# Hybrid mLSTM and sparse-attention block: another order for the attention step, the compressed branch spread out, 32 small sums moved to GpSimd

## The chip, the core and the metric

The kernel runs on one core of one Trainium2 chip. The metric is device time in microseconds of one execution; less is better. Three runs of the kernel before gave 2147.64, 2150.17 and 2151.10 us, median 2150.17 us. One further execution was recorded by the hardware profiler, and all rows below come from it.

## The reference, cut to what matters

One layer over 256 tokens of width 4096. A wide projection gives the inputs of an mLSTM half and of an attention half; their outputs, gated, go through `w_out`, are added to `x`, and a second gated product is added.

```python
def reference(x, p, norm_w, w_in, ..., w_out, ple_proj, ple_gate):
    h = _rmsnorm(x, norm_w[layer])
    u = h @ w_in[layer]
    ...
    y_ml = hm.reshape(B, S, ML_WIDTH) * jax.nn.sigmoid(ml_o) * jax.nn.silu(ml_z)
    y_ns = _nsa(ns_q, ns_kc, ns_vc, ns_ks, ns_vs, ns_kw, ns_vw, ns_g, ...) * jax.nn.silu(ns_z)
    x = x + jnp.concatenate([y_ml, y_ns], axis=-1) @ w_out[layer]
    x = x + jax.nn.sigmoid(x @ ple_gate[layer]) * (p[layer] @ ple_proj[layer])
```

The attention half (`_nsa`) has 4 groups of 4 heads of width 128. Every query attends three times: to 15 compressed blocks (`sc`, `p_c`, `o_c`), to selected blocks (with 256 tokens all 4 blocks of 64 are selected) and to a window (512, so it too reaches back over all tokens). The three results are added with gates:

```python
    blk = jnp.concatenate([seg[:, :-1], seg[:, 1:]], axis=2) + pe[:, None, :]   # _compress
    ...
    sc = jnp.einsum('bsghd,bcgd->bghsc', qg, kcmp) * scale + bias_c
    p_c = _masked_softmax(sc, dist_c >= 0)
    o_c = jnp.einsum('bghsc,bcgd->bsghd', p_c, vcmp)
    ...
    s = jnp.einsum('bqghd,bgqkd->bghqk', qb, kg) * scale + bias
    pr = _masked_softmax(s, ...)
    ...
    o = gs[..., 0:1] * o_c + gs[..., 1:2] * o_s + gs[..., 2:3] * o_w
```

## The kernel before, in words

The kernel is one long list of units. A unit is one 512 KB weight tile (`raw`, 128x1024 numbers) loaded by SyncE's queue and the matmuls that use it. To keep nearly full precision a tile is split in two: ScalarE writes its high part (`whi`, L1478), VectorE subtracts that from the tile and writes the low part (`wlo`, L1479). A unit of the kind "wide" (L912 to L914) is 12 matmuls of 512 columns: two blocks, two halves of the tokens, three products of high and low parts. Other units ("pair", L1191) use a scheme with fewer products that needs sums of neighbouring weight tiles on VectorE (L1276 to L1280, `raw<-raw`).

The main loop at the end of the program goes through the units in order. In iteration n it first splits unit n+3 (`LOOK` is 3; `whi` and `wlo` have four buffers each), then runs what was put off in `behind`, then issues the matmuls of unit n, then takes one step of each of the queues of generators: `urgent`, `fifo`, and `dry`. All side work (attention, mLSTM, norms, tables) is written as such generators, one step per `yield`. Engines run their instructions in the order of the program, so the place of a step between the units is the place of its instructions on every engine.

The attention of one group is the generator `t_nq`. After the norm it runs 11 steps, one per unit. The eight attention units of the group are the pairs (head h, half t of the queries); t = 0 sees 128 keys, t = 1 sees 256, both for two branches (selected and window) side by side. In step i come, on TensorE, the scores of attention unit i (L582 to L584, into the one PSUM bank `sd0`), the transposes of unit i-2 (L616, into `sd1`), and the products with the values of unit i-3 (L629, into `sd2` for t = 0 and `sd3` for t = 1); on VectorE the bias is added to the scores (L592, it reads `sd0`, so the next scores wait for it), their maximum taken (L594), and the transposed weights of unit i-2 copied (L621); on ScalarE the exponential (L599). `coef` (L604, L605, VectorE) and `scale` (L609, ScalarE) of unit i are put into `behind`: they follow the next iteration's split. Small biased tables `tb` come by DMAs issued on GpSimd's queue (L521).

The compressed branch is a generator inside (`compressed`, L537 to L575): eight small score products into `sd3` (L540), a block-diagonal tile `bd` of the compressed values (cleared by GpSimd, L543, filled by four ScalarE copies, L557), a softmax on VectorE (L548 to L566), two transposes (L571) and at the end one product per half (L632).

Elsewhere `t_xp` (L310) adds the position table `pe` to the transposed inputs of the compression, in 32 VectorE additions of 128x120 numbers, for the 16 units whose matmuls stand in L1004. `t_stat` (L817 and after) turns finished activations into stationary tiles; its `pause` says how many steps pass before the first transposes.

Of the kernel before, what the change touches and what calls it, by code (L numbers as in the profile page):

```python
# [21 lines left out]
NCMP = 15  # L22
# [65 lines left out]
def hymba_block(ctx: ExitStack, tc: tile.TileContext, a, out: bass.AP):  # L88
# [209 lines left out]
    def t_xp():  # L298
        while "ct" not in done:
            yield "wait"  # L300
        for q in range(4):
            if q % 2 == 0:
                both_q = wk.tile([128, 2, 8, 120], F32, tag=f"nat{q // 2}", name="xq")
            xq[q] = both_q[:, q % 2]
            for kv in range(2):
                o = 16 * (q // 2)
                v = held[f"c{kv}"][:, :, o:o + 240].rearrange("p g (b l) -> p g b l", l=16)
                l0 = 8 * (q % 2)
                for g in range(4):
                    nc.vector.tensor_tensor(  # L310
                        xq[q][:, :, kv * 60 + g * 15:kv * 60 + (g + 1) * 15].rearrange("p l b -> p b l"),
                        v[:, g, :, l0:l0 + 8],
                        pe[:, kv, None, 8 * q:8 * q + 8].to_broadcast([128, 15, 8]), op=OP.add)
                if kv:
                    done.add(f"xq{q}")
                yield
# [184 lines left out]
    def t_nq(flag, g):  # L501
# [8 lines left out]
        for t in range(2):  # L510
            r = slice(t * 128, (t + 1) * 128)
            nc.scalar.activation(qh[:, :, r], pp[t], AF.Copy)
            nc.vector.tensor_sub(ql[:, :, r], pp[t], qh[:, :, r])
        units = [(h, t) for t in range(2) for h in range(4)]
        tb = {}

        def load_tb(i):
            h, t = units[i]
            n = 128 * (t + 1)
            tb[i] = wk.tile([128, n], F32, tag="tb", name="tb", bufs=3)  # L520
            nc.gpsimd.dma_start(tb[i], bass.AP(tensor=rext_d.tensor, offset=rext_d.offset + (4 * g + h) * 384 + 1,  # L521
                                               ap=[[1, 128], [1, n]]))

        for i in range(2):
            load_tb(i)
        yield
# [9 lines left out]
        def compressed():  # L536
            pc = side(3, [128, 8, NCMP])  # L537
            for t in range(2):
                for h in range(4):
                    MM(pc[:, 4 * t + h, :], qt[:, h, t * 128:(t + 1) * 128], kct[:, g, :], start=True, stop=True)  # L540
            yield
            bd = cm["bd"] = sqtile([128, 4, 128])
            nc.gpsimd.memset(bd, 0.0)  # L543
            sc = small([128, 8, 32], "sc", 1)
            nc.gpsimd.memset(sc, 0.0)
            scv = sc[:, :, 0:NCMP]
            for t in range(2):
                nc.vector.tensor_tensor(scv[:, 4 * t:4 * t + 4], pc[:, 4 * t:4 * t + 4],  # L548
                                        biasc[:, 8 - 8 * t:23 - 8 * t, 4 * g:4 * g + 4].rearrange("p c h -> p h c"), op=OP.add)
            m8 = small([128, 8], "mx8")  # L550
            nc.vector.tensor_reduce(m8, scv, axis=AX.X, op=OP.max)
            nc.vector.tensor_tensor(scv, scv, m8[:, :, None].to_broadcast([128, 8, NCMP]), op=OP.subtract)
            yield
            nc.scalar.activation(scv, scv, AF.Exp)
            for h in range(4):
                r = slice(32 * h, 32 * h + 32)
                nc.scalar.activation(bd[r, h, :], vcmp[r, g, :], AF.Copy)  # L557
            yield
            sm = small([128, 8], "sm8")
            nc.vector.tensor_reduce(sm, scv, axis=AX.X, op=OP.add)  # L560
            nc.vector.reciprocal(sm, sm)
            nc.vector.tensor_tensor(sm.rearrange("p (t h) -> p t h", t=2), sm.rearrange("p (t h) -> p t h", t=2),
                                    sg4[:, :, 4 * g:4 * g + 4, 0], op=OP.mult)
            nc.vector.tensor_tensor(scv, scv, sm[:, :, None].to_broadcast([128, 8, NCMP]), op=OP.mult)
            for t in range(2):
# [3 lines left out]
            pp = side(3, [128, 2, 128])  # L569
            for t in range(2):  # L570
                nc.tensor.transpose(pp[:, t, :], sc[:, 4 * t:4 * t + 4, :].rearrange("p h c -> p (h c)"), idn)  # L571
            yield
            pct = cm["pct"] = small([128, 2, 128], "pct", 1)
            nc.vector.tensor_copy(pct, pp)
            yield  # L575

        def scores(i):
            h, t = units[i]
            n = 128 * (t + 1)
            psd[i] = side(0, [128, 2, n])  # L580
            r = slice(t * 128, (t + 1) * 128)
            MM(psd[i], qh[:, h, r], kh[:, g, :, 0:n], start=True, stop=False)  # L582
            MM(psd[i], ql[:, h, r], kh[:, g, :, 0:n], start=False, stop=False)
            MM(psd[i], qh[:, h, r], kl[:, g, :, 0:n], start=False, stop=True)  # L584
            if i + 2 < 8:
                load_tb(i + 2)

        def bias_max(i):
            h, t = units[i]
            n = 128 * (t + 1)  # L590
            sb[i] = stile([128, 2, n])
            nc.vector.tensor_tensor(sb[i], psd[i], tb.pop(i)[:, n - 1::-1][:, None, :].to_broadcast([128, 2, n]), op=OP.add)  # L592
            mx[i] = small([128, 2], "mx2", 3)
# [17 lines left out]
        def trans(i):  # L611
            h, t = units[i]
            psd[i] = side(1, [128, 2, t + 1, 128])
            for b in range(2):
                for s in range(t + 1):
                    nc.tensor.transpose(psd[i][:, b, s, :], sb[i][:, b, s * 128:(s + 1) * 128], idn)  # L616

        def copy_pt(i):
            h, t = units[i]
            ptb[i] = pttile([128, 2, t + 1, 128])  # L620
            nc.vector.tensor_copy(ptb[i], psd[i])  # L621

# [20 lines left out]
        for i in range(11):  # L643
# [288 lines left out]
    def add(*gens):  # L932
        fifo.extend(gens)
# [260 lines left out]
    def pair_group(g, w, stat):  # L1194
# [48 lines left out]
        def new_activations(g, chunks, b):  # L1243

            if g < 0:
                add(t_stat([(c, (c * 512 + 2048) % 4096, f"p1_{c}", f"y{c}") for c in chunks], range(16), b, pace=1 + b, pause=1 - b))
            else:
                add(t_stat([(c, c * 512, f"p2_{c}", f"r{c}") for c in chunks], (), b, pace=1 + b, pause=1 - b))
            if b:
# [204 lines left out]

    raws, splits = {}, {}

# [12 lines left out]

    held_raw = [0]  # L1470

# [11 lines left out]
    def split_one(r):  # L1483
# [3 lines left out]
        return hi, lo  # L1487

    def split(n):
        r = raws.pop(n, None)  # L1490
        if n == 0:
# [39 lines left out]
    for n in range(N):  # L1531
        un = units[n]
        late = un.get("late")
# [105 lines left out]
```

## Time and profile before

| | |
|---|---|
| median of three runs | 2150.17 us (2147.64 to 2151.10) |
| the profiled execution's own time | 2147.24 us |
| its span in the profile | 2145.5 us |
| granted TensorE clock, mean | 0.998 of full speed |
| TensorE matmuls busy | 2114.0 us, 99% |
| VectorE busy | 1727.4 us, 81% |
| ScalarE busy | 1218.3 us, 57% |
| GpSimd busy | 42.7 us, 2% |

The time lies 1.74 us above the span. A busy TensorE in this profile has modelled ends: a short matmul's record lasts 0.28 us, while matmuls of 128 columns can pass every 0.11 us, so a record that ends late can hide a piece of a wait. In the rows, `sd<-kh,qh` names the output and inputs of an instruction, "[1.96 <-DVE s L592]" the idle time before it and who ended it.

### The profile page before, as it was taken

The page shows a single profiled execution, that of the slowest core. Times are in us where ns is not written, and L with a number is a line of the kernel's source. Part 1 is how long each engine was busy: PE and PEld are TensorE (multiplying, and loading weights), DVE is VectorE, ACT ScalarE, POOL GpSimd, SP SyncE. Part 2 cuts the span into 40 slices and gives each one's busy share as a digit, 9 for nine tenths or more (in the row PEclk, how much of TensorE's full clock was granted, in tenths as well). Part 3 has the DMA queues.
Part 4 walks back from the last instruction along what each step waited for, and adds up shares of the span by engine and source line. Part 5 has one row for each costly group of instructions (what it writes and reads, how often), then busy time and mean ns, then how long its engine had stood idle before and what let it go on. Part 6 is the DMA issues. An engine that isn't in the chain of part 4 may idle for free.

```text
span 2145.5 us, 27052 instructions
## 1 busy us (share of the span) xinstructions
PE 2114.0 (99%) x9655; PEld 1732.8 (81%) x9655; DVE 1727.4 (81%) x2246; ACT 1218.3 (57%) x1573; POOL 42.7 (2%) x90
## 2 busy tenths in 40 slices
PE   9999999999999999999999999999999999999998
PEld 7877788877777888888888888888888888888887
DVE  7885699566565767869999899888998986988888
ACT  7654455555555555565655556565555555555554
POOL 1000000010000000000000000000000000000000
PEclk9999999999999999999999999999999999999999
DMA  9646756554444455665566566556665665566664
GB/s 370 220 157 233 247 197 208 195 169 145 135 139 147 144 182 177 188 204 177 186 212 223 175 206 220 198 201 241 204 225 179 213 217 167 198 204 221 203 216 145
DMA packets 118759, 423.14 MB, mean 197 GB/s; under 512 B 13906, under 2 KB 14218, under 8 KB 118624
## 3 DMA queue, kind: packets, MB, share of 16 engines
q1 hardware_dynamic: 114272, 409.00, 56.6%
q0 software_dynamic: 4208, 12.40, 2.0%
q8 instruction: 76, 1.25, 0.2%
q14 instruction: 59, 0.48, 0.1%
q10 hardware_dynamic: 144, 0.02, 0.0%
HBM read 417.13 MB, written 4.23 MB: 196 GB/s over the span
## 4 chain that ended last, share of the span: by engine, by line
PE 90%; DVE 6%; ACT 3%; issue 1%; ACTq 0%; DVEq 0%
PE mm L1191 44%; PE sd L1191 28%; PE mm L912 8%; PE mm L914 4%; DVE wlo L1479 3%; ACT whi L1478 1%; ACT s L599 1%; DVE mx L594 1%; PE sd L1004 1%; DVE s L592 1%; PE sd L817 1%; PE sd L629 0%; PE sd L279 0%; PE sd L616 0%; DVE xq L310 0%
## 5 line engine op out<-in xcount | busy, mean ns | idle before, releaser
L1479 DVE TENSOR_TENSOR wlo<-raw,whi 128x1024 fp32r<-128x1024 f32 x848 | 1029.6, 1221 | 353.0 <-ACT whi L1478 338.7
L1478 ACT ACTIVATE whi<-raw 128x1024 fp32r<-128x1024 f32 x848 | 890.2, 1059 | 692.4 <-PE mm L1191 164.9
L1191 PE MATMUL mm<-whi,sh 128*128 128x512 f32 x1221 | 395.2, 393 | 1.4 <-DVE vsw L1092 0.5
L1191 PE MATMUL mm<-wlo,sh 128*128 128x512 f32 x1221 | 390.4, 390 | 1.0 <-DVE wlo L1479 1.0
L1191 PE MATMUL mm<-whi,sl 128*128 128x512 f32 x1221 | 390.4, 390 | 0.0
L1191 PEld LDWEIGHTS mm<-wlo,sh 128*128 128x128 f32 x1221 | 229.3, 188 | 50.2 <-DVE wlo L1479 2.7
L1191 PEld LDWEIGHTS mm<-whi,sh 128*128 128x128 f32 x1221 | 227.5, 188 | 52.3 <-issue 4.1
L1191 PEld LDWEIGHTS mm<-whi,sl 128*128 128x128 f32 x1221 | 229.7, 188 | 48.4
L1191 PE MATMUL sd<-whi,sh 128*128 128x512 f32 x686 | 225.3, 390 | 0.0
L1191 PE MATMUL sd<-whi,sl 128*128 128x512 f32 x686 | 224.9, 389 | 0.0
L1191 PE MATMUL sd<-wlo,sh 128*128 128x512 f32 x686 | 224.9, 389 | 0.0
L912 PE MATMUL mm<-whi,sh 128*128 128x512 f32 x512 | 166.9, 407 | 0.3 <-DVE mv L1092 0.3
L912 PE MATMUL mm<-whi,sl 128*128 128x512 f32 x512 | 158.8, 392 | 0.0
L914 PE MATMUL mm<-wlo,sh 128*128 128x512 f32 x512 | 158.2, 390 | 0.0
L1191 PEld LDWEIGHTS sd<-whi,sl 128*128 128x128 f32 x686 | 128.9, 188 | 27.0
L1191 PEld LDWEIGHTS sd<-wlo,sh 128*128 128x128 f32 x686 | 128.9, 188 | 26.9
L1191 PEld LDWEIGHTS sd<-whi,sh 128*128 128x128 f32 x686 | 128.6, 188 | 26.8
L1191 PE MATMUL sd<-whi,cb 128*128 128x512 f32 x450 | 146.8, 391 | 0.0
L1191 PE MATMUL mm<-whi,cb 128*128 128x512 f32 x390 | 130.7, 391 | 0.0
L914 PEld LDWEIGHTS mm<-wlo,sh 128*128 128x128 f32 x512 | 96.4, 188 | 20.9
L912 PEld LDWEIGHTS mm<-whi,sl 128*128 128x128 f32 x512 | 96.4, 188 | 20.8
L912 PEld LDWEIGHTS mm<-whi,sh 128*128 128x128 f32 x512 | 92.8, 189 | 20.3 <-issue 3.8
(325 smaller groups left out, 1975.7 us busy)
## 6 DMA issues: line engine op xcount, KB each, us to landing
raw<-in_w_gate SPq DMA_DIRECT2D x192, 512.0 KB, 4.2
raw<-in_w_ip SPq DMA_DIRECT2D x159, 512.0 KB, 4.3
raw<-in_w_in SPq DMA_DIRECT2D x128, 512.0 KB, 3.5
raw<-in_w_out SPq DMA_DIRECT2D x128, 512.0 KB, 4.2
raw<-in_ple_gate SPq DMA_DIRECT2D x128, 512.0 KB, 3.5
raw<-in_w SPq DMA_DIRECT2D x16, 512.0 KB, 4.6
u<-in_xt SPq DMA_DIRECT2D x16, 256.0 KB, 7.9
xn<-in_x SPq DMA_DIRECT2D x4, 1024.0 KB, 6.3
```

The costliest lines, as they stand in the source:

```text
L592: nc.vector.tensor_tensor(sb[i], psd[i], tb.pop(i)[:, n - 1::-1][:, None, :].to_broadcast([128, 2, n]), op=OP.add)
L594: nc.vector.tensor_reduce(mx[i], sb[i], axis=AX.X, op=OP.max, negate=True)
L599: nc.scalar.activation(sb[i][:, b], sb[i][:, b], AF.Exp, bias=mx[i][:, b:b + 1], accum_out=sums[i][:, b:b + 1])
L817: nc.tensor.transpose(pp[i // 2][:, i % 2, t * 128:(t + 1) * 128], src[:, t, k:k + 128], idn)
L912: MM(box["ps"][t], s[c][:, k, t * 128:(t + 1) * 128], m[:, j, :], start=st, stop=False)
L914: MM(box["ps"][t], sh[c][:, k, t * 128:(t + 1) * 128], lo[:, j, :], start=False, stop=last)
L1004: MM(o[64 * kv:64 * kv + 60], xq[l // 8][:, l % 8, 60 * kv:60 * kv + 60], raw[:, j, 256 * kv:256 * kv + 256], start=(l == 0), stop=(l == 31))
L1191: MM(acc.t, s, m, start=acc.i == 0, stop=acc.i == acc.n - 1)
L1478: nc.scalar.activation(hi, r, AF.Copy)
L1479: nc.vector.tensor_sub(lo, r, hi)
```

## The change

In `t_nq`:

- The order of attention units is now (h, t) with t fastest, so half 0 and half 1 alternate. The outputs of both halves are complete only at the end: `out_t(0)` moves from step 6 to step 9.
- `tb` is one table of 256 columns per head, used by both halves: four DMAs per group in place of eight.
- In each step a new `split_hi` stands ahead of `bias_max`: ScalarE writes the high part of the unit that the next iteration will split (n+4), ahead of the exponential of the step. `split` finds it done and only subtracts on VectorE, which then comes behind the step's maximum.
- `compressed`: its scores go into the free columns of the score bank of step 0 (`psd[0]`), its transposes into the free columns of step 6's transposes (`psd[4]`); `bd` is filled by four DMAs on GpSimd's queue in place of four ScalarE copies; clearing of `bd` and `sc` and the bias additions move from step 1 to step 0, and the other operations spread over steps 1 to 6.

Elsewhere: the 32 additions of `t_xp` run on GpSimd, and `pause` is 2 in place of 1 for the first two chunks of `t_stat`.

```diff
@@ t_xp
-                    nc.vector.tensor_tensor(
+                    nc.gpsimd.tensor_tensor(
@@ t_nq
-        units = [(h, t) for t in range(2) for h in range(4)]
+        units = [(h, t) for h in range(4) for t in range(2)]
...
+        def load_tb(h):
+            tb[h] = wk.tile([128, 256], F32, tag="tb", name="tb", bufs=3)
...
         def compressed():
-            pc = side(3, [128, 8, NCMP])
+            pc = psd[0][:, 256:256 + 8 * NCMP].rearrange("p (h c) -> p h c", c=NCMP)
...
-            yield
             bd = cm["bd"] = sqtile([128, 4, 128])
             nc.gpsimd.memset(bd, 0.0)
+            for h in range(4):
+                r = slice(32 * h, 32 * h + 32)
+                nc.gpsimd.dma_start(bd[r, h, :], vcmp[r, g, :])
             sc = small([128, 8, 32], "sc", 1)
             nc.gpsimd.memset(sc, 0.0)
...
             nc.scalar.activation(scv, scv, AF.Exp)
-            for h in range(4):
-                r = slice(32 * h, 32 * h + 32)
-                nc.scalar.activation(bd[r, h, :], vcmp[r, g, :], AF.Copy)
...
             at(pv, i - 3)
+            split_hi(now[0] + 1 + LOOK)
             at(bias_max, i)
...
-            if i == 6:
+            if i == 9:
@@ new_activations (both calls of t_stat)
-   pause=1 - b
+   pause=2 - 2 * b
@@ the main loop's helpers
+    def split_hi(n):
+        if n < N and units[n]["kind"] == "wide":
+            r = raws.pop(n)
+            ahead[n] = (r, *split_tiles())
+            nc.scalar.activation(ahead[n][1], r, AF.Copy)
+
     def split(n):
+        if n in ahead:
+            r, hi, lo = ahead.pop(n)
+            nc.vector.tensor_sub(lo, r, hi)
+            held_raw[0] -= 1
+            splits[n] = (hi, lo)
+            return
```

Where the instructions stand now. First ScalarE at the start of a group's attention steps; `whi` is the high part of a weight tile, L599 the exponential, L609 the scaling. Before:

```order
L599 ACTIVATE s,sm_3826<-s,mx_3824 128x128 x2
L1478 ACTIVATE whi<-raw 128x1024
L609 ACTIVATE s<-s,sm_3826 128x128 x2
L599 ACTIVATE s,sm_3870<-s,mx_3868 128x128 x2
L1478 ACTIVATE whi<-raw 128x1024
L609 ACTIVATE s<-s,sm_3870 128x128 x2
L554 ACTIVATE sc<-sc 128x8x15
L557 ACTIVATE sq<-vcmp 32x128 x4
L599 ACTIVATE s,sm_3915<-s,mx_3911 128x128 x2
L1478 ACTIVATE whi<-raw 128x1024
```

Now, at the same place (L1494 is the high part written ahead):

```order
L1494 ACTIVATE whi<-raw 128x1024
L599 ACT_TABLE_LOAD
L599 ACTIVATE s,sm_3839<-s,mx_3837 128x128 x2
L609 ACTIVATE s<-s,sm_3839 128x128 x2
L1494 ACTIVATE whi<-raw 128x1024
L599 ACTIVATE s,sm_3874<-s,mx_3872 128x256 x2
L609 ACTIVATE s<-s,sm_3874 128x256 x2
L555 ACTIVATE sc<-sc 128x8x15
L1494 ACTIVATE whi<-raw 128x1024
L599 ACTIVATE s,sm_3915<-s,mx_3911 128x128 x2
```

The high part now stands ahead of each exponential, the four copies from `vcmp` are gone, and exponentials of 128 and of 256 columns alternate.

VectorE at the same place; L592 adds the bias to the scores, L594 is the maximum, `sc` belongs to the compressed branch. Before:

```order
L1479 TENSOR_TENSOR wlo<-raw,whi 128x1024
L592 TENSOR_TENSOR s<-sd_3807,tb 128x256
L594 TENSOR_REDUCE mx_3824<-s 128x2
L1479 TENSOR_TENSOR wlo<-raw,whi 128x1024
L604 RECIPROCAL sm_3826<-sm_3826 128x2
L605 TENSOR_TENSOR sm_3826<-sm_3826,sg 128x2
L548 TENSOR_TENSOR sc<-sd_3813,biasc 128x4x15 x2
```

Now:

```order
L1480 TENSOR_TENSOR wlo<-raw,whi 128x1024
L548 TENSOR_TENSOR sc<-sd_3807,biasc 128x4x15 x2
L592 TENSOR_TENSOR s<-sd_3807,tb 128x256
L594 TENSOR_REDUCE mx_3837<-s 128x2
L1499 TENSOR_TENSOR wlo<-raw,whi 128x1024
L604 RECIPROCAL sm_3839<-sm_3839 128x2
L605 TENSOR_TENSOR sm_3839<-sm_3839,sg 128x2
```

The two bias additions of the compressed branch (L548) moved ahead of the bias addition of step 0 (L592), and read the same PSUM buffer as it.

GpSimd from the constants to the start of the first group; `xq` are the 32 small sums, `sq` is `bd`. Here the lines of the difference, those of the kernel before with a minus:

```order
 L162 MEMSET biasc 128x128
+L310 TENSOR_TENSOR xq<-ct,pe_c 128x15x8 x32
 L249 DMA oh<-in_onehot 33x864
...
-L521 DMA tb<-rext_d 128x128 x4
-L543 MEMSET sq 128x512
+L519 DMA tb<-rext_d 128x256 x3
+L540 MEMSET sq 128x512
+L543 DMA sq<-vcmp 32x128 x4
 L545 MEMSET sc 128x256
```

GpSimd now clears `bd`, issues four DMAs, and only then clears `sc`, into which the additions L548 of VectorE write.

## Rows read from the trace of the kernel before

**Rows 1.** Part 1 of the page: busy time, share of the span and instructions of each engine.

```profile
PE 2114.0 (99%) x9655; PEld 1732.8 (81%) x9655; DVE 1727.4 (81%) x2246; ACT 1218.3 (57%) x1573; POOL 42.7 (2%) x90
```

**Rows 2.** The table of stretches, 50 us in the middle of the first attention group: start and end, length, busy time of each engine with its instructions, granted clock, DMA share, GB/s.

```profile
450.00:500.00 50.00, 45.52 (x238) 36.63 (x237) 29.70 (x62) 29.00 (x68) 5.06 (x10) 1.00 0.42 132
```

**Rows 3.** The waits of TensorE over the whole span: who waited for whom, us in total, times, longest.

```profile
PE sd L582 <- DVE s L592: 10.6, 8, 2.3
PE sd L616 <- ACT s L599: 5.2, 5, 1.2
...
PE sd L616 <- DVE pt L621: 1.1, 6, 0.2
...
PE mm L817 <- DVE u L1120: 0.6, 1, 0.6
PE mm L817 <- DVE s L1033: 0.6, 1, 0.6
```

**Rows 4.** The timeline of one step of the first group, from the copies into `bd` on ScalarE to the next scores on TensorE: start, length, engine, line, operation, count and the idle time before it.

```profile
469.87 1.25 ACT L557 ACTIVATE sq<-vcmp 32x128 f32<-32x128 f32 x4
471.14 0.40 ACT L599 ACTIVATE s<-s,mx 128x128 f32<-128x128 f32 x1
...
471.93 1.04 ACT L1478 ACTIVATE whi<-raw 128x1024 fp32r<-128x1024 f32 x1
...
473.00 1.22 DVE L1479 TENSOR_TENSOR wlo<-raw,whi 128x1024 fp32r<-128x1024 f32 x1 [2.90 <-ACT whi L1478]
...
475.75 0.41 DVE L592 TENSOR_TENSOR s<-sd,tb 128x256 f32<-128x256 f32 x1
...
476.22 0.50 PE L582 MATMUL sd<-kh,qh 128*128 128x512 f32 x1 [1.96 <-DVE s L592]
```

**Rows 5.** The timeline of TensorE at the starts of attention steps: the first group from its first scores (L582) to its last product (L632), then two steps of the fourth group; and the bias addition's durations (shortest, median, longest in ns).

```profile
459.01 0.28 PE L582 MATMUL sd<-kh,qh 128*128 128x256 f32 x1
...
463.92 0.28 PE L582 MATMUL sd<-kh,qh 128*128 128x256 f32 x1
...
467.01 0.28 PE L582 MATMUL sd<-kh,qh 128*128 128x256 f32 x1
...
470.33 0.28 PE L582 MATMUL sd<-kh,qh 128*128 128x256 f32 x1
...
470.91 0.61 PE L629 MATMUL sd<-vsw,pt 128*128 128x128 f32 x4
...
498.51 0.63 PE L616 MATMUL sd<-idn,s 128*128 128x128 f32 x4 [1.16 <-ACT s L599]
...
502.61 0.60 PE L616 MATMUL sd<-idn,s 128*128 128x128 f32 x4
...
507.61 1.02 PE L632 MATMUL sd<-sq,pct 128*128 128x512 f32 x2
...
699.25 0.39 PE L582 MATMUL sd<-kh,qh 128*128 128x512 f32 x1
...
703.38 0.39 PE L582 MATMUL sd<-kh,qh 128*128 128x512 f32 x1
...
708.62 0.39 PE L582 MATMUL sd<-kh,qh 128*128 128x512 f32 x1
...
L592 DVE TENSOR_TENSOR s<-sd,tb x32: 411/550/692, 459.6 to 712.7; 128x256 f32<-128x256 f32 x16, 128x512 f32<-128x512 f32 x16
```

**Rows 6.** The timeline of GpSimd at three places (a DMA behind a clearing at the start, three DMAs in a row, the clearing of `bd` and `sc`), the compressed scores on TensorE, and the bias additions of the compressed branch on VectorE, all in the first group but the first row.

```profile
1.84 0.67 POOL L147 DMA_DIRECT2D rel<-in_rel  x1 [0.32 <-POOL rel L146]
...
430.34 1.65 POOL L521 DMA_DIRECT2D tb<-rext_d  x3
...
459.36 1.85 PE L540 MATMUL sd<-kct,sq 128*128 128x15 f32 x16
...
461.37 0.53 POOL L543 MEMSET sq<- 128x512 f32 x1 [0.55 <-ACT s L599]
461.83 0.31 POOL L545 MEMSET sc<- 128x256 f32 x1
...
463.75 0.42 DVE L548 TENSOR_TENSOR sc<-sd,biasc 128x60 f32<-128x60 f32 x2
```

**Rows 7.** The stage of the small sums: the sums themselves (instructions by line, 129 to 147 us), the same 18 us in the table of stretches, the low parts just before (106 to 129 us, idle time and who ended it), TensorE's waits from 129 to 171 us, the copies into `ct` that the sums read, the first ScalarE instruction that reuses a buffer of `ct`, the matmuls that read `xq` (first and last start), and the one GpSimd instruction before that reads and writes.

```profile
L310 DVE TENSOR_TENSOR xq<-ct,pe_c 128x120 f32<-128x120 f32 x32 | 8.6, 399 | 0.0
...
129.00:147.00 18.00, 17.10 (x73) 13.12 (x72) 17.93 (x45) 9.13 (x10) 0.00 (x0) 1.00 0.46 150
...
L1479 DVE TENSOR_TENSOR wlo<-raw,whi 128x1024 fp32r<-128x1024 f32 x7 | 8.6, 1224 | 6.3 <-ACT whi L1478 6.3
...
PE mm L1191 <- DVE wlo L1479: 1.0, 3, 0.5
PE sd L1191 <- DVE wlo L1479: 0.7, 2, 0.4
...
L292 DVE COPY ct<-sd x2: 682/682/683, 99.9 to 105.3; 128x512 f32<-128x512 f32 x2
...
151.07 0.63 ACT L804 ACTIVATE cb<-s 128x512 fp32r<-128x512 f32 x1 [3.89 <-DVE s L800]
...
L1004 PE MATMUL sd<-raw,xq x128: 379/379/427, 191.8 to 231.8; 128*60 128x256 f32 x128
...
1.02 0.29 POOL masks.py:199 TENSOR_SCALAR_AFFINE_SELECT idn<-idn 128x128 f32<-128x128 f32 x1
```

More of the change, by code (lines that the diff above doesn't have):

```diff
@@ L513, in t_nq @@
             nc.vector.tensor_sub(ql[:, :, r], pp[t], qh[:, :, r])
-        units = [(h, t) for t in range(2) for h in range(4)]
+        units = [(h, t) for h in range(4) for t in range(2)]
         tb = {}
[L517 to L525, printed above, removed]
+        def load_tb(h):
+            tb[h] = wk.tile([128, 256], F32, tag="tb", name="tb", bufs=3)
+            nc.gpsimd.dma_start(tb[h], bass.AP(tensor=rext_d.tensor, offset=rext_d.offset + (4 * g + h) * 384 + 1,
+                                               ap=[[1, 128], [1, 256]]))
+        for h in range(2):
+            load_tb(h)
         yield
@@ L550, in compressed @@
             m8 = small([128, 8], "mx8")
+            yield
             nc.vector.tensor_reduce(m8, scv, axis=AX.X, op=OP.max)
@@ L563, in compressed @@
                                     sg4[:, :, 4 * g:4 * g + 4, 0], op=OP.mult)
+            yield
             nc.vector.tensor_tensor(scv, scv, sm[:, :, None].to_broadcast([128, 8, NCMP]), op=OP.mult)
+            yield
             for t in range(2):
@@ L568, in compressed @@
             yield
-            pp = side(3, [128, 2, 128])
             for t in range(2):
-                nc.tensor.transpose(pp[:, t, :], sc[:, 4 * t:4 * t + 4, :].rearrange("p h c -> p (h c)"), idn)
-            yield
+                nc.tensor.transpose(psd[4][:, 2 + t, :], sc[:, 4 * t:4 * t + 4, :].rearrange("p h c -> p (h c)"), idn)
             pct = cm["pct"] = small([128, 2, 128], "pct", 1)
-            nc.vector.tensor_copy(pct, pp)
+            nc.vector.tensor_copy(pct, psd[4][:, 2:4, :])
             yield
@@ L579, in scores @@
             n = 128 * (t + 1)
-            psd[i] = side(0, [128, 2, n])
+            psd[i] = side(0, [128, 512])
+            ps = psd[i][:, 0:2 * n].rearrange("p (b k) -> p b k", b=2)
             r = slice(t * 128, (t + 1) * 128)
[L582 to L586, printed above, removed]
+            MM(ps, qh[:, h, r], kh[:, g, :, 0:n], start=True, stop=False)
+            MM(ps, ql[:, h, r], kh[:, g, :, 0:n], start=False, stop=False)
+            MM(ps, qh[:, h, r], kl[:, g, :, 0:n], start=False, stop=True)
+            if t == 0 and h + 2 < 4:
+                load_tb(h + 2)
         def bias_max(i):
@@ L591, in bias_max @@
             sb[i] = stile([128, 2, n])
-            nc.vector.tensor_tensor(sb[i], psd[i], tb.pop(i)[:, n - 1::-1][:, None, :].to_broadcast([128, 2, n]), op=OP.add)
+            ps = psd[i][:, 0:2 * n].rearrange("p (b k) -> p b k", b=2)
+            nc.vector.tensor_tensor(sb[i], ps, tb[h][:, n - 1::-1][:, None, :].to_broadcast([128, 2, n]), op=OP.add)
             mx[i] = small([128, 2], "mx2", 3)
@@ L612, in trans @@
             h, t = units[i]
-            psd[i] = side(1, [128, 2, t + 1, 128])
+            psd[i] = side(1, [128, 4, 128])
             for b in range(2):
                 for s in range(t + 1):
-                    nc.tensor.transpose(psd[i][:, b, s, :], sb[i][:, b, s * 128:(s + 1) * 128], idn)
+                    nc.tensor.transpose(psd[i][:, (t + 1) * b + s, :], sb[i][:, b, s * 128:(s + 1) * 128], idn)
         def copy_pt(i):
@@ L620, in copy_pt @@
             ptb[i] = pttile([128, 2, t + 1, 128])
-            nc.vector.tensor_copy(ptb[i], psd[i])
+            nc.vector.tensor_copy(ptb[i].rearrange("p b s k -> p (b s) k"), psd[i][:, 0:2 * t + 2])
         def pv(i):
@@ L1245, in new_activations @@
             if g < 0:
-                add(t_stat([(c, (c * 512 + 2048) % 4096, f"p1_{c}", f"y{c}") for c in chunks], range(16), b, pace=1 + b, pause=1 - b))
+                add(t_stat([(c, (c * 512 + 2048) % 4096, f"p1_{c}", f"y{c}") for c in chunks], range(16), b, pace=1 + b, pause=2 - 2 * b))
             else:
-                add(t_stat([(c, c * 512, f"p2_{c}", f"r{c}") for c in chunks], (), b, pace=1 + b, pause=1 - b))
+                add(t_stat([(c, c * 512, f"p2_{c}", f"r{c}") for c in chunks], (), b, pace=1 + b, pause=2 - 2 * b))
             if b:
@@ L1452, in hymba_block @@
         pair_group(g, a["ple_gate"][g - 4], "r")
-    raws, splits = {}, {}
+    raws, splits, ahead = {}, {}, {}
     def load(n):
@@ L1468, in load @@
             nc.sync.dma_start(raws[n], units[n]["src"])
-    held_raw = [0]
+    held_raw, now = [0], [0]
     def split_tiles():
@@ L1531, in hymba_block @@
     for n in range(N):
-        un = units[n]
+        un, now[0] = units[n], n
         late = un.get("late")
```

## The prediction

> **What bounds the kernel now.** I read the page's first part, then the stretches, then TensorE's waits, then the timeline at those waits. TensorE is busy 2114.0 of 2145.5 us [rows 1]: it is the bound, and all that can be won without less work for it is its 31 idle us and what its records hide. The reader is to see that these are not spread evenly: 4.5 of the 50 us in the middle of the first attention group are idle [rows 2]. The waits say for what. TensorE waits 10.6 us for the bias addition L592 before the next scores, 5.2 us for ScalarE and 1.1 us for the copy L621 before the transposes: 16.9 us in 19 waits, all in the four attention groups [rows 3]. The rest of the kernel waits little, and nowhere in a place that this change touches but for 1.7 us in the stage of the small sums [rows 7] and twice 0.6 us at the new stationary tiles [rows 3].
>
> **Why TensorE waits there.** One step shows it [rows 4]. ScalarE finishes the copies into `bd` at 471.1, then the exponential, and only then, at 471.93, the high part of the next weight tile. VectorE stood idle 2.90 us for it, subtracts the low part at 473.00, does the small sums, and reaches the bias addition at 475.75; the scores, which need its bank, start at 476.22. So the ring is bias, maximum, exponential, high part, low part, bias: two engines by turns, each idle while the other works. In this ring VectorE is not full.
>
> What a group loses to it: from its first scores at 459.01 to its last product at 507.61 it takes 48.60 us [rows 5]. Without waits I build it from steps that have none. Step 0 takes 4.91 (459.01 to 463.92), step 1 3.09, step 2 3.32. A pass of 128 columns costs (0.61-0.28)/3 = 0.11, so step 3 with four passes of values is 3.76. A step with 256 keys in the scores, 128 in transposes and values is 4.13 (699.25 to 703.38); step 4 has two transposes more, 4.35; step 5 is 4.13; step 6, with the two products L632, 5.24 (703.38 to 708.62); step 7 with two transposes and four passes more 4.79; steps 8 and 9 are 4.10 each (498.51 to 502.61), the last eight passes 0.88. Sum 42.67. So a group loses 5.93 us, four lose 23.7. The rows of waits show 16.9 of them; a late end of a record hides some 0.17 of each wait (0.28 against 0.11), 3 us, and the rest I can't place. The gain possible is between 16.9 and 23.7; I take 23.7, since it comes from starts and not from modelled ends.
>
> **The high part ahead, the low part behind the maximum.** No instruction is added. ScalarE writes the high part as soon as unit n's matmuls free a buffer, which is before the step's scores end; it takes 1.04 [rows 4], while VectorE adds the bias and takes the maximum, 0.41 and about as much for 128 keys, 0.69 twice for 256 [rows 5]. So the exponential behind it is not later. After the maximum VectorE copies (0.41 to 0.69), subtracts (1.22, rows 4), and finds the exponential's sums done. Per step VectorE then needs 2.8 us for t = 0, 3.6 for t = 1, and some 0.3 for the compressed branch; TensorE needs 3.1 to 5.2. TensorE is late last in every step but one, and the ring is gone: -23.7 us. Alternating halves costs and gains nothing by itself (TensorE has the same passes); it keeps four steps of 3.6 from standing in a row. The half-width DMAs of `tb` that go leave GpSimd's queue, where nothing waits for them.
>
> **The step that gets a new wait: step 0.** L548 now stands ahead of the bias addition L592 on VectorE and writes into `sc`, which GpSimd clears behind the four new DMAs. The chain: `bd` can be cleared when the compressed scores, which start at 459.36 and last 1.85, have read `qt`, whose buffer it takes; as before at 461.37, until 461.90 [rows 6]. A DMA behind a clearing came 0.32 later, and DMAs in a row take 1.65/3 = 0.55 each [rows 6]: 462.2 to 464.4. Clearing `sc` 0.31, 464.7; L548 0.42, then L592 0.41: 465.6. The scores of step 1 need that bank and could start at 463.92 [rows 5]. So they are 1.7 us late, four times: +6.8 us. Behind it the step's maximum, the low part and the following bias addition shift too; I followed them to step 3 and find each bias addition 0.3 to 0.9 us ahead of the scores that need its bank. The low part delayed there is for a unit that runs three units later. No DMA of 32 rows with 512 bytes stands in the trace: from below this wait is worth 0 (if clearing and DMAs overlapped fully), from above 3.6 us with DMAs of twice the length; I take the nearest rows, 0.55.
>
> The four copies gone from ScalarE (1.25 per group) and the spread of the softmax are part of the ring above and give nothing more. The table load in front of the exponential now follows the high part; step 0's wait covers it.
>
> **The small sums on GpSimd.** VectorE is busy 17.93 of the 18 us in which it does them, 8.6 us of it sums, and from 129 to 171 us TensorE waits 1.7 us for low parts [rows 7]. Without the sums these waits go: -1.7 us. On GpSimd all 32 stand in one row and wait only for `ct`, ready at 106 us. ScalarE needs the buffer of `ct` back at 151.07, after 28 sums; TensorE needs the first `xq` at 191.8 [rows 7]. That leaves 45/28 = 1.6 us per sum. What a sum costs on GpSimd no row shows; the nearest, with one input and 128 columns, is 0.29 [rows 7]; from above I allow 2.0. I take 0.5: nothing waits.
>
> A rule speaks against this part: the Trainium skill, "SBUF — State Buffer", section "Who interferes with whom", says that a VectorE instruction with two inputs in SBUF and a GpSimd instruction that reads SBUF block each other for a whole instruction. No row of before has such a pair, so the trace neither bears it out nor refutes it.
>
> As a mechanism of this kernel: if each sum held a VectorE instruction up for 0.5 us, that would be 16 us between 106 and 147; VectorE has 6.3 idle us there until 129 and 8.6 freed after it [rows 7], 14.9 in all. The waits would stay or grow a little.
>
> **The pause.** Two first transposes L817 waited 0.6 us each for VectorE [rows 3]; 12 or so matmuls later the data is there: -1.2 us. The tiles are needed only when the next group of units starts, and the order leaves units in between.
>
> **Sum.** -23.7 + 6.8 - 1.7 - 1.2 = -19.8 us. The profiled execution's own time was 2147.24, which gives 2127.4; the median of the runs is 2.9 above it, and on it, 2150.17 - 19.8 = 2130.4. I predict 2130 us.
>
> **Rivals.** (a) The chain on GpSimd in step 0 is dearer. For it: no DMA from SBUF to SBUF was ever timed here, and four have to be issued before `sc` is cleared. With 1.1 us each the scores are 3.9 late, +15.6: a gain of 11, 2139. (b) The chain costs nothing, because clearing and issuing overlap: 2150.17 - 26.6 = 2123.6. Against it: three DMAs in a row took 1.65 us, three times one [rows 6]. (c) GpSimd and VectorE block each other: 1.7 not won and up to 3 lost, 2132 to 2135. (d) Slower than before: a sum on GpSimd takes so long that ScalarE stands in front of `cb` and writes no high parts. ScalarE is then free at 106 + 28c; TensorE has three units in hand, 5 us by an estimate from step 1 of rows 5 (3.09 less the scores leaves 2.7 for a unit of 12 matmuls; the units here have 3 to 12), so the loss is 28c - 50. The gain of 19.8 is used up at c = 2.5 us; at c = 3.2 the loss is 40 and the time 2170. For it: 32 instructions with scattered writes on an engine never seen doing such; against it: 0.29 for a larger tile with one input. (e) The ring isn't cut, because ScalarE's high part waits for a buffer: `whi` has four, and unit n+4 takes that of unit n. It is cut in the order of instructions, since unit n's matmuls come ahead of the step on TensorE too; half the gain would be 2142.
>
> **Chances.** Forecast 0.62, (a) 0.13, (b) 0.08, (c) 0.08, (d) 0.04, (e) 0.05. The range, 2121 to 2142 us, holds the forecast, (b), (c) and (a). About 0.2% (4.3 us) is what can be told from no change. Only (d), and bad mixtures of (a), (c) and (e), reach that: faster 0.93, same 0.03, slower 0.04.
>
> **What would show it.** In the profile after, first scores to last product of a group should take 44.4 us in place of 48.6. TensorE's waits for L592 should be four, one per group at step 1, of 1.4 to 1.7 us, with VectorE idle before L548 for GpSimd's clearing of `sc`; those for ScalarE before transposes near 0. VectorE should no longer be idle for high parts in steps 1 to 7. The four DMAs should stand 0.55 apart. The 32 sums should be over before 150 us, and TensorE's waits for low parts between 129 and 171 gone. Wrong would be: waits of 2 us and more still at the fourth scores of a group (the ring lives), waits in steps 2 to 4 (step 0's delay is not made up), or ScalarE standing at `cb` for GpSimd.

## The result and the profile after

The changed kernel takes 2126.47 us, the median of four runs (2125.48 to 2128.33), the kernel before 2149.07 us on the same chip (2147.64 to 2151.10): ratio 0.9895, 95% interval 0.9878 to 0.9912, 22.6 us less. The prediction was 2130 us with a range of 2121 to 2142, faster with a chance of 0.93. The profiled execution took 2126.45 us with a span of 2124.4; before it was 2147.24 and 2145.5. The two spans are 21.1 us apart, and below I account for those.

Part 1 of the page and the stretch of 50 us in the middle of the first group, kernel after, as [rows 1] and [rows 2]:

```profile
PE 2105.7 (99%) x9655; PEld 1734.0 (82%) x9655; DVE 1724.9 (81%) x2214; ACT 1214.8 (57%) x1557; POOL 66.9 (3%) x122
...
450.00:500.00 50.00, 48.59 (x259) 40.96 (x258) 33.21 (x68) 28.84 (x65) 5.02 (x10) 1.00 0.45 143
```

VectorE and ScalarE do nearly the same work as before. In the stretch TensorE is idle 1.4 us in place of 4.5, and 259 matmuls fall into it in place of 238. GpSimd gained 24 us of work, almost all of it small sums.

The waits of TensorE over the whole span, kernel after, as [rows 3]:

```profile
PE sd L581 <- DVE s L592: 5.3, 4, 1.4
...
PE sd L616 <- ACT s L599: 0.3, 1, 0.3
```

Of 16.9 us for bias additions, exponentials and copies 5.6 are left, and 5.3 of these are one wait per group. The two waits at L817 (now L818) are gone. TensorE's starts in the first group, kernel after, scores (L581) and last product (L632), as [rows 5]:

```profile
456.97 0.28 PE L581 MATMUL sd<-kh,qh 128*128 128x256 f32 x1
463.45 0.47 PE L581 MATMUL sd<-kh,qh 128*128 128x512 f32 x1 [1.41 <-DVE s L592]
466.97 0.28 PE L581 MATMUL sd<-kh,qh 128*128 128x256 f32 x1
...
501.18 1.02 PE L632 MATMUL sd<-sq,pct 128*128 128x512 f32 x2
```

The group takes 501.18 - 456.97 = 44.21 us; the other three take 44.10, 44.68 and 44.07, where before it was 48.60, 48.62, 48.60 and 48.52. That is 17.3 us in four groups. From these starts and those of other lines the span divides so: the first scores stand at 456.97 in place of 459.01 (2.0 us won ahead of attention), the last product of the fourth group at 704.60 in place of 723.91 (17.3 more), and the last instruction 21.1 earlier (1.8 more, behind attention).

How a step runs now shows the timeline of the fourth step of the first group, with the low part before it, kernel after, as [rows 4]:

```profile
470.69 1.23 DVE L1499 TENSOR_TENSOR wlo<-raw,whi 128x1024 fp32r<-128x1024 f32 x1 [1.05 <-ACT whi L1494]
...
472.73 0.68 DVE L592 TENSOR_TENSOR s<-sd,tb 128x512 f32<-128x512 f32 x1
...
472.88 1.04 ACT L1494 ACTIVATE whi<-raw 128x1024 fp32r<-128x1024 f32 x1
...
473.45 0.69 DVE L594 TENSOR_REDUCE mx<-s 128x2 f32<-128x512 f32 x1
...
474.05 0.68 DVE L621 COPY pt<-sd 128x512 f32<-128x512 f32 x1
474.17 0.51 ACT L599 ACTIVATE s<-s,mx 128x256 f32<-128x256 f32 x1 [0.24 <-DVE mx L594]
...
474.63 0.28 PE L581 MATMUL sd<-kh,qh 128*128 128x256 f32 x1
474.65 1.22 DVE L1499 TENSOR_TENSOR wlo<-raw,whi 128x1024 fp32r<-128x1024 f32 x1
```

ScalarE writes the next high part (L1494) while VectorE adds the bias and takes the maximum; the exponential follows the maximum by 0.03, and the low part (L1499) follows the copy without a gap. The scores at 474.63 come 1.2 us after the bias addition that freed their bank.

The wait that is left, at the second scores of the first group, kernel after, from the compressed scores on:

```profile
457.32 1.85 PE L538 MATMUL sd<-kct,sq 128*128 128x15 f32 x16
...
459.39 0.53 POOL L540 MEMSET sq<- 128x512 f32 x1 [29.44 <-PE sd L538]
...
460.21 2.00 POOL L543 DMA_DIRECT2D sq<-vcmp  x4 [0.29 <-POOL sq L540]
...
462.19 0.33 POOL L545 MEMSET sc<- 128x256 f32 x1
462.56 0.41 DVE L548 TENSOR_TENSOR sc<-sd,biasc 128x60 f32<-128x60 f32 x2 [6.19 <-POOL sc L545]
462.88 0.42 DVE L592 TENSOR_TENSOR s<-sd,tb 128x256 f32<-128x256 f32 x1
```

Line by line this is the chain of the prediction: clearing `bd`, four DMAs of 0.50 us each, clearing `sc`, then the two bias additions, and only then the scores at 463.45. VectorE stood idle 6.19 us for it.

### The profile page after: what moved, and what is told of

The parts are those of the page before. It is cut to its first block, busy times and chain, and to the rows that moved or that the text cites. A ratio compares the mean times of both kernels' runs of the same rounds, so it can differ in the third digit from the quotient of the medians.

```text
span 2124.4 us, 27026 instructions
## 1 busy us (share of the span) xinstructions
PE 2105.7 (99%) x9655; PEld 1734.0 (82%) x9655; DVE 1724.9 (81%) x2214; ACT 1214.8 (57%) x1557; POOL 66.9 (3%) x122
## 4 chain that ended last, share of the span: by engine, by line
PE 96%; DVE 2%; POOL 1%; issue 1%; ACT 0%; DMA 0%; SPq 0%; DVEq 0%; ACTq 0%; POOLq 0%
PE mm L1192 44%; PE sd L1192 29%; PE mm L913 10%; PE mm L915 5%; PE sd L629 1%; DVE wlo L1480 1%; PE sd L1005 1%; PE sd L818 1%; PE sd L279 0%; PE sd L616 0%; POOL sq L543 0%; PE sd L632 0%; PE sd L538 0%; DMA raw<-in_w_ip 0%; PE sd L581 0%
## 5 line engine op out<-in xcount | busy, mean ns | idle before, releaser
L1479 ACT ACTIVATE whi<-raw 128x1024 fp32r<-128x1024 f32 x804 | 845.3, 1059 | 694.6 <-PE mm L1192 163.0
L1480 DVE TENSOR_TENSOR wlo<-raw,whi 128x1024 fp32r<-128x1024 f32 x804 | 978.2, 1224 | 278.0 <-ACT whi L1479 261.2
```

The lines of the kernel that those rows point to most:

```text
L1479: nc.scalar.activation(hi, r, AF.Copy)
L1480: nc.vector.tensor_sub(lo, r, hi)
```

## The experiments

Seven kernels ran, each beside the kernel before. None leaves work out.

### 1. The high part ahead, alone

The kernel before with one edit of the change: the call in the step, with what it needs in the splitting.

```diff
             at(pv, i - 3)
+            split_hi(now[0] + 1 + LOOK)
             at(bias_max, i)
```

> The kernel before with one thing of the change: the high part of the next tile ahead of the exponential, its low part behind the maximum. Halves in the old order, compressed branch, small sums and pause as before. Theory (the ring of VectorE and ScalarE is the whole loss, and this edit alone cuts it): the first group's 48.60 us from first scores to last product fall to 42.7 to 44.5, with what is left at the step where the old compressed branch puts its softmax and four copies in one place; the time is 2131 to 2133 us. Rival (the alternation of the halves or the spread of the compressed branch is what gives VectorE room): a group still takes over 46 us, waits for the bias addition remain at the fourth scores and in the steps of 256 keys, and the time is over 2138 us.

Measured: 2124.22 us (2123.98 to 2125.30), ratio 0.9883 (0.9868 to 0.9898), beside 2149.33 for before. The expectation named the right side, but its time of 2131 to 2133 us was 7 us too high: the wait that it left for the old compressed branch is not there. The whole gain is in this edit. By the groups it is more than the whole; by time alone that is not settled, since the intervals of this ratio and of the changed kernel's overlap. The first two scores of the first group, and its last product:

```profile
460.20 0.28 PE L582 MATMUL sd<-kh,qh 128*128 128x256 f32 x1
465.11 0.28 PE L582 MATMUL sd<-kh,qh 128*128 128x256 f32 x1
...
502.78 1.02 PE L632 MATMUL sd<-sq,pct 128*128 128x512 f32 x2
```

The group takes 42.58 us, the others 42.57, 42.56 and 42.56; the prediction built 42.67 for a group without waits. No scores or transposes wait any more, though the halves stand as before, four of one kind and then four of the other, and ScalarE still copies into `bd`. The ring alone was worth 194.34 - 170.27 = 24.1 us in the four groups. The one call moves two instructions, the high part ahead of the exponential on ScalarE and the low part behind the maximum on VectorE; no run moves one without the other.

### 2. Everything but the high part ahead

```diff
             at(pv, i - 3)
-            split_hi(now[0] + 1 + LOOK)
             at(bias_max, i)
```

> The changed kernel without the high part ahead: ScalarE writes it again in the next iteration, behind the exponential. Everything else of the change stays. Theory: the ring is back, a group takes 47 to 49 us (it also keeps the new wait of step 0), the time is 2138 to 2146 us. Rival (alternation and spread carry the gain): a group takes 44 to 45.5 us and the time is 2126 to 2131 us.

Measured: 2156.05 us (2155.29 to 2157.59), ratio 1.0030 (1.0018 to 1.0043): slower than before by 6.7 us. The theory's 2138 to 2146 us and its groups of 47 to 49 us were both too low. Its waits of TensorE:

```profile
PE sd L581 <- DVE s L592: 17.4, 16, 1.7
PE sd L616 <- ACT s L599: 10.4, 12, 1.1
```

The ring lives, and a group takes 51.86, 51.76, 51.71 and 51.18 us, 3 more than before. The scores wait in four steps of every group. Why the new order costs more where the ring is left is what experiment 7 asks.

### 3. The scores' buffer cleared first

The changed kernel with the clearing of `sc` moved ahead of the clearing of `bd` and its DMAs.

```diff
+            sc = small([128, 8, 32], "sc", 1)
+            nc.gpsimd.memset(sc, 0.0)
             bd = cm["bd"] = sqtile([128, 4, 128])
             nc.gpsimd.memset(bd, 0.0)
             for h in range(4):
                 r = slice(32 * h, 32 * h + 32)
                 nc.gpsimd.dma_start(bd[r, h, :], vcmp[r, g, :])
-            sc = small([128, 8, 32], "sc", 1)
-            nc.gpsimd.memset(sc, 0.0)
```

> The changed kernel with one instruction moved on GpSimd: sc is cleared ahead of bd and of the four DMAs. Theory (the scores of step 1 wait for the chain clearing of bd, four DMAs, clearing of sc, bias additions): the wait of 1.4 us before the second scores of each group goes, the first group takes 42.6 to 42.8 us in place of 44.21, and the time falls by 6 us to about 2120 us. Rival (the wait comes from the shared bank of the scores and the compressed scores, or from the additions themselves): the second scores still wait over 0.8 us, and the time stays above 2123 us.

Measured: 2120.79 us (2119.16 to 2121.57), ratio 0.9865 (0.9850 to 0.9880). The same place in the first group:

```profile
459.30 0.28 PE L581 MATMUL sd<-kh,qh 128*128 128x256 f32 x1
...
461.62 0.42 DVE L548 TENSOR_TENSOR sc<-sd,biasc 128x60 f32<-128x60 f32 x2 [2.92 <-PE sd L538]
...
461.96 0.42 DVE L592 TENSOR_TENSOR s<-sd,tb 128x256 f32<-128x256 f32 x1
...
462.54 2.00 POOL L545 DMA_DIRECT2D sq<-vcmp  x4 [0.29 <-POOL sq L542]
...
464.21 0.39 PE L581 MATMUL sd<-kh,qh 128*128 128x512 f32 x1
```

L548 now waits for the compressed scores alone and runs ahead of the DMAs, and the second scores come 4.91 us after the first, as in the kernel before. Groups take 42.52, 42.52, 42.51 and 42.50: 170.05 in place of 177.06. So the chain on GpSimd cost 7.0 us in the four groups. By time this kernel is 5.7 us below the changed one, by span 4.7, because it reaches its first scores 2.3 us later (459.30 against 456.97; the last section says why).

### 4. The sums back on VectorE

```diff
-                    nc.gpsimd.tensor_tensor(
+                    nc.vector.tensor_tensor(
                         xq[q][:, :, kv * 60 + g * 15:kv * 60 + (g + 1) * 15].rearrange("p l b -> p b l"),
```

> The changed kernel with the 32 small sums back on VectorE. Theory (VectorE was full in that stage and GpSimd relieves it, although each of its sums lengthens VectorE's instructions of two SBUF inputs by 0.24 us): low parts between 100 and 127 us last 1.22 again, the first matmul with xq starts 3.3 us later (191.8), part of it is made up in the stage behind, where weight tiles arrive late, so the first attention scores come 2 us later and the time is 2128 to 2129 us. Rival (what the sums free they cost again by blocking, and the difference seen is only another phase): the first scores move by less than 0.7 us and the time stays at 2126 to 2127 us.

Measured: 2129.79 us (2129.19 to 2131.67), ratio 0.9909 (0.9894 to 0.9924), 3.3 us above the changed kernel; the intervals of the two ratios overlap, so the sign rests on the trace. There TensorE's waits for low parts are back (1.0 and 0.9 us).

What the sums are worth has to be read from a start that lies ahead of them, because the profiles reach this stage at different times, though no edit acts ahead of it: VectorE's first copy into `ct` (L292) starts at 99.84 in the changed kernel and at 100.80 here. From this copy to the first matmul that reads `xq` it takes 91.8 to 91.9 us in the three kernels with the sums on VectorE (before, 1 and 4) and 88.7 in the six with the sums on GpSimd: 3.1 to 3.2 us in every pair. Of the 2.9 us by which the first scores of the attention come later here (459.88 against 456.97), 1.0 stands ahead of the sums; the sums make 1.9 of it.

### 5. The short pause

```diff
-... range(16), b, pace=1 + b, pause=2 - 2 * b))
+... range(16), b, pace=1 + b, pause=1 - b))
```

(and the same in the line below it)

> The changed kernel with the two pauses set back to 1 - b. If the second slot of pause is what took the two 0.6 us waits away before the rows at 1434 and 1776 us, the kernel gets 1.2 to 1.8 us longer than the changed one, 2127.7 to 2128.3 us, and the two waits of TensorE for the row's sums are back at about 0.6 us each. Rival: those waits went because the attention steps leave other work at other places, and the pause does nothing: 2126.5 us, no waits.

Measured: 2128.42 us (2127.26 to 2130.32), ratio 0.9903 (0.9889 to 0.9916). By time alone it can't be told from the changed kernel, but two waits of its list can:

```profile
PE mm L818 <- DVE u L1121: 0.6, 1, 0.6
PE mm L818 <- DVE s L1034: 0.6, 1, 0.6
```

From the end of the fourth group to the second row of L818 transposes this kernel takes 710.2 + 342.3 us (705.27 to 1415.5 to 1757.8), as the kernel before does (723.91 to 1434.1 to 1776.4); the changed kernel takes 709.5 + 341.3 (704.60 to 1414.1 to 1755.4). So the pause is worth 0.7 + 1.0 = 1.7 us.

### 6. Three edits alone

Experiment 1 with the sums on GpSimd and the long pause; the order of the halves, the compressed branch and its ScalarE copies stay as before.

> The kernel before with three edits alone: the high part ahead of the exponential, the 32 sums on GpSimd, the longer pause. The order of the units, the compressed branch, its copies on ScalarE and its clearing stay as before. If the alternating halves, the spread branch and the four DMAs bring nothing by themselves, it takes the 2124.2 us of the high part alone less 2 to 3.3 for the sums less 1.2 to 1.8 for the pause: 2119 to 2121 us, the same as the changed kernel with the scores' buffer cleared first (2120.8), with groups of 42.6 us. Rival: the spread and the alternation free VectorE for the other branches and are worth 1 us or more: 2122 us or above.

Measured: 2120.99 us (2119.20 to 2121.53), ratio 0.9866 (0.9853 to 0.9879), the same as experiment 3, with the same span of 2119.7 and groups of 42.57, 42.57, 42.56 and 42.56. Alternating halves, spreading the branch and filling `bd` by DMAs are together worth nothing, once `sc` is cleared in time.

### 7. The ring, with the scores' buffer cleared first

Experiments 2 and 3 together.

> The changed kernel without the high part ahead, and with the buffer of the compressed scores cleared ahead of the block-diagonal one and its four DMAs. It asks why the changed kernel without the high part ahead took 2156.1 us, 6.7 above the kernel before. If that is the wait behind the GpSimd chain, 1.5 us in each of four groups put on top of the ring of VectorE and ScalarE, it goes with the chain: 2149 to 2150.5 us, groups of about 50.3 us, no wait at the second scores. Rival: the ring swallows what is saved at its start, since its steps are limited by VectorE and ScalarE and not by when TensorE starts: 2154 to 2156 us, the waits at later scores longer.

Measured: 2142.68 us (2142.35 to 2146.51), ratio 0.9974 (0.9964 to 0.9984). Both theories missed: the clearing is worth 13.4 us here, not 6 and not nothing. Groups take 48.63, 48.63, 48.59 and 48.01 us, as in the kernel before (48.60), and 12.7 less in all than in experiment 2. VectorE's bias addition, set against the first scores, shows what happened. Experiment 2, first scores and step 0 on VectorE:

```profile
458.49 0.28 PE L581 MATMUL sd<-kh,qh 128*128 128x256 f32 x1
...
464.09 0.41 DVE L548 TENSOR_TENSOR sc<-sd,biasc 128x60 f32<-128x60 f32 x2 [6.20 <-POOL sc L545]
464.41 0.42 DVE L592 TENSOR_TENSOR s<-sd,tb 128x256 f32<-128x256 f32 x1
```

And experiment 7:

```profile
456.14 0.28 PE L581 MATMUL sd<-kh,qh 128*128 128x256 f32 x1
...
458.46 0.42 DVE L548 TENSOR_TENSOR sc<-sd,biasc 128x60 f32<-128x60 f32 x2 [2.92 <-PE sd L538]
458.80 0.41 DVE L592 TENSOR_TENSOR s<-sd,tb 128x256 f32<-128x256 f32 x1
```

The bias addition comes 5.92 us after the first scores in the one and 2.66 in the other. The group differs by 3.23 us (51.86 against 48.63), that is by the whole delay of 3.26 on VectorE, not by the 1.57 that TensorE waits at the second scores. The delay lasts to the end of the group: counted from the first scores, each of the seven bias additions behind it comes 3.25 to 3.27 us later in experiment 2 than in experiment 7. With the ring cut, in the changed kernel against experiment 3, the same delay on VectorE (5.91 against 2.66) shrinks from one bias addition to the last, from 3.25 to 1.69, and the group is 1.69 longer (44.21 against 42.52), 1.57 of it at the second scores. So in the ring, where VectorE and ScalarE wait for each other by turns, VectorE did not make up what it was late. That the ring itself is the reason is argued from these starts; no run of its own was made for it.

The kernel before shows the other side. In its fourth group TensorE's granted clock falls to half, 1.2 of 2.4 GHz, right behind a wait of 2.34 us for the bias addition:

```profile
694.00:695.00 1.00, 1.00 (x8) 1.00 (x8) 0.00 (x0) 1.00 (x5) 0.00 (x0) 0.70 0.31 53
695.00:696.00 1.00, 1.00 (x5) 0.90 (x5) 0.54 (x1) 0.43 (x1) 0.00 (x0) 0.50 0.57 74
```

(The third number from the end is the granted clock.) From these scores to the next, 693.11 to 699.25, it takes 6.14 us, 1.6 more than at the same place of the third group (4.53). Yet the group takes 48.52 us, like the others: the two steps behind take 4.13 and 5.24 in place of 5.30 and 5.68, because TensorE, late itself, no longer waits there. In the ring 1.6 us of TensorE cost nothing.

## Why the prediction was right

**What bounds the kernel, and the ring.** Right. TensorE was the bound, and the idle time in four groups was the thing to win. The term was -23.7 us; experiment 1 measures 24.1 for the edit by itself. Building a group from steps without waits (42.67) hit what a group without waits takes (42.50 to 42.58). Two of those steps, 699.25 to 703.38 and 703.38 to 708.62, were without waits in the fourth group alone, behind the fall of the clock told under experiment 7; that they could be read at all was luck.

**Alternating halves costs and gains nothing by itself.** Right for its own cost: experiments 3 and 6 have one span, experiment 7 and the kernel before one group. But the prediction added that it keeps four long steps from standing in a row, as if that helped: it doesn't. In experiment 1 the four steps with 256 keys stand in a row and nothing waits.

**The new wait in step 0.** Right in mechanism; that the sizes agree so closely is in part luck. Predicted +6.8 us, 1.7 each; experiment 3 takes away 7.0. The trace has each link. The DMAs took 0.50 (496 to 521 ns in 16) where I took 0.55, so the low bound (nothing) and the high one (3.6) are both out. (The one single DMA of [rows 6] took 0.67, so three in a row were not three times one, as is said against rival (b).) But the second scores come only 1.57 us late in the first group and 1.45 to 1.46 in the others, 5.9 in all. The other 1.1 us is lost in later steps, 0.7 of it in the third group, where TensorE waits 0.3 us for an exponential; the prediction put nothing there.

**The small sums.** Right in sign; the size has to be read with care. The chip gave 2.0 us at the first scores of the attention against 1.7 predicted, but by two errors that go against each other. First, the wait that went was larger: the start of the matmuls on `xq` moved by 3.3 us (191.8 to 188.5), while the 1.7 us of [rows 7] were taken from matmul rows. The same waits read from the weight loads before those matmuls are 4.5 us, so what was lost lies between the two readings. Kernel before, waits of the loads from 129 to 171 us:

```profile
PEld mm L1191 <- DVE wlo L1479: 2.7, 4, 0.9
...
PEld sd L1191 <- DVE wlo L1479: 1.8, 3, 0.8
```

Second, 1.2 us was given back behind it, 0.7 of that at 236 us, where TensorE now arrives before ScalarE and VectorE are done. Kernel after:

```profile
236.18 1.31 PE L279 MATMUL sd<-idn,u 128*128 128x128 f32 x8 [0.74 <-DVE kl L417]
```

It need not be given back: experiment 7 has no such wait, and from the first matmul on `xq` to the first scores it takes 267.2 us, as the kernel before does; the changed kernel takes 268.5. A sum took longer on GpSimd than the 0.5 us taken, median 0.74, yet all were over by 127.6, well ahead of 150. Kernel after, the sums by line and in time:

```profile
L310 POOL TENSOR_TENSOR xq<-ct,pe_c x32: 442/742/1433, 100.7 to 126.7; 128x120 f32<-128x120 f32 x32
...
106.68 20.89 POOL L310 TENSOR_TENSOR xq<-ct,pe_c 128x120 f32<-128x120 f32 x28 [2.35 <-DVE ct L292]
```

**The pause.** Right: 1.2 predicted, 1.7 to 1.8 measured. Again the waits listed for the matmuls, 1.2 us together, were less than what was lost.

**The sum.** -24.1 + 7.0 - 2.0 - 1.8 = -20.9, beside -23.7 + 6.8 - 1.7 - 1.2 = -19.8 predicted and a difference of the spans of 21.1. Only the first two of these four terms are measured apart from that difference: their 17.1 stands beside 17.3 in the groups, while 2.0 and 1.8 are pieces of the 21.1 itself, for which experiments 4 and 5 give 1.9 and 1.7. The median is 22.6 lower, 1.5 more than the spans, because the profiled execution of the kernel before was 1.8 faster than that kernel's median. The time came out 3.5 under the forecast: the gain was 2.8 larger than the sum and the kernel before 1.1 faster than the 2150.17 that I started from, less 0.4 for rounding down to 2130.

**The marks.** Of the seven, six came as told: groups of 44.2 (44.4), four waits at step 1 (one of 1.41 and three of 1.30 where I had 1.4 to 1.7), transposes waiting 0.3, the DMAs in a row, the sums over in time, no waits for low parts from 129 to 171 us. One did not: VectorE still stands idle for high parts at times, 1.05 us at 470.69 in the first group (first row of the step shown above). It delays nothing, since TensorE is late last there.

**The rivals.** (a) and (b), a dearer and a free chain, fall with experiment 3: 7.0 us, not 15.6 or nothing. (e), the ring not cut, falls with experiment 1. (d), ScalarE held up by slow sums, falls with their 0.74 us, far under 2.5. (c), GpSimd and VectorE blocking each other, is there but small, 0.5 us: see the last section.

## What to carry to other kernels

Where TensorE waits for two engines that pass work to and fro, look for the one instruction in the ring that depends on neither, and issue it while the other engine works: here one call gave 24 us, and the rest of a larger change took back some of it. A clearing that another engine needs soon goes first in its queue, ahead of DMAs that nobody waits for yet. Here a delay of 3.26 us on VectorE cost 3.23 in a group with the ring and 1.69 in one without, and 1.6 us of a slower TensorE cost nothing with the ring: so price a delay for the kernel with the other edits in.

## What the runs showed of the hardware that I had not expected

**VectorE beside GpSimd.** While the sums run on GpSimd, VectorE's instructions with two inputs in SBUF get longer. Low parts between 99 and 128 us, shortest, median and longest, kernel after, and one addition of two tiles of 128x512:

```profile
L1480 DVE TENSOR_TENSOR wlo<-raw,whi x9: 1217/1410/1521, 98.7 to 124.0; 128x1024 fp32r<-128x1024 f32 x9
...
109.38 0.92 DVE L795 TENSOR_TENSOR s<-sh,sl 128x512 f32<-128x512 f32 x1
```

Kernel before, the same:

```profile
L1479 DVE TENSOR_TENSOR wlo<-raw,whi x10: 1215/1224/1226, 98.8 to 126.7; 128x1024 fp32r<-128x1024 f32 x10
...
108.57 0.68 DVE L794 TENSOR_TENSOR s<-sh,sl 128x512 f32<-128x512 f32 x1
```

Each gets about 0.2 us longer, and a sum on GpSimd lies between 0.44 and 1.43. The copy L320 between them, whose one input lies in PSUM, stays at 0.41. So the rule of the Trainium skill, "SBUF — State Buffer", section "Who interferes with whom", by which such a pair blocks each other, agrees with this trace in direction. Over all 32 sums VectorE's instructions got some 4.5 us longer (an estimate, added up from the timelines of before and after), where the prediction's 0.5 per sum makes 16. TensorE felt it in one place. At 103 us it waits for the copy L320, which now comes behind two longer instructions; kernel before and kernel after:

```profile
103.30 0.50 PE L1191 MATMUL mm<-whi,sh 128*128 128x512 f32 x1 [0.45 <-DVE sq L320]
...
103.75 0.50 PE L1192 MATMUL mm<-whi,sh 128*128 128x512 f32 x1 [0.95 <-DVE sq L320]
```

This wait is 0.9 in all six kernels with the sums on GpSimd and 0.4 to 0.5 in the three others: 0.5 us lost, within the 3.2 won.

**TensorE's clock near 200 us.** In experiments 2, 3, 5 and 6 the granted clock falls to half, 1.2 of 2.4 GHz, for about 3.5 us; in the kernels before and after and in 1, 4 and 7 it stays at 1.00 there. The table of stretches of 1 us, its third number from the end the granted clock, experiment 3:

```profile
199.00:200.00 1.00, 1.00 (x10) 0.78 (x11) 0.38 (x2) 0.33 (x1) 0.00 (x0) 0.77 0.42 90
200.00:201.00 1.00, 1.00 (x8) 0.45 (x4) 1.00 (x2) 0.73 (x1) 0.00 (x0) 0.50 0.95 360
```

What TensorE did before it fell, experiment 3, and the matmuls that then ran at half speed:

```profile
198.30 1.28 PE L260 MATMUL sd<-rel,oh 33*128 33x16 f32 x10
199.52 1.97 PE L1005 MATMUL sd<-raw,xq 128*60 128x256 f32 x8
201.41 1.22 PE L1192 MATMUL mm<-whi,sh 128*128 128x512 f32 x2
```

The kernel after issues the same instructions there, with the same eight matmuls of L1005:

```profile
197.53 1.29 PE L260 MATMUL sd<-rel,oh 33*128 33x16 f32 x10
198.75 1.08 PE L1005 MATMUL sd<-raw,xq 128*60 128x256 f32 x8
```

Ahead of the fall stand, in both, groups of ten matmuls of 16 columns (L260), and no wait of TensorE. From the last such group to the third product behind it experiment 3 takes 4.85 us (198.30 to 203.15), the kernel after 3.26 (197.53 to 200.79): the fall cost 1.6 us. With 0.8 that stand ahead of the sums already (100.62 against 99.84 at the first copy into `ct`) that is the 2.3 us by which experiment 3 reaches its first scores later than the changed kernel, and it hides that much of what the edit of experiment 3 is worth in time. In this study the clock fell near 200 us only with the sums on GpSimd, in four of six profiles; what decides between two kernels that issue the same instructions here is open, and so is whether it fell in the runs that had no profile.
